# Token-tile gate loads, the first spectrum's row fix and Fourier's negated rows behind the filters' squares, in a one-layer Fourier and Hyena block

## The chip, the cores and the metric

The kernel runs on one core of one Trainium2 chip. The metric is the device time of one execution in microseconds (us). All arithmetic is in 32-bit floats; products that need full precision are made of three matmuls on a high and a low part of each operand.

TensorE (PE in the profile; PEld is its weight load), VectorE (DVE), ScalarE (ACT) and GpSimd (POOL) each work through a queue of their own, in order. Nearly all transfers are issued from the queue of SyncE (SP).

## The reference

One layer on x of 2048 tokens by 1024 channels, cut to what matters here:

```python
p = rmsnorm(x, g_mix) @ w_in                     # 512 Fourier channels, 3 x 512 Hyena channels
y_f = rmsnorm(fourier_mix(p[..., :512]), g_fourier)   # real part of a 2-D FFT, 8 groups of 64
u = short_conv(p[..., 512:])                     # 3 taps along the tokens
x1, x2, v = split(u, 3)
k = implicit_filters(...)                        # 2 orders x 512 channels, length 4096:
                                                 #   k * rsqrt(sum(k * k) + EPS)
k_freq = rfft(k)
z = v
for n, gate in enumerate((x1, x2)):
    z = gate * fft_long_conv(z, k_freq[:, n], long_d[n])
y_h = rmsnorm(z, g_hyena)
x = x + concat(y_f, y_h) @ w_out
x = x + square(relu(rmsnorm(x) @ w_fc1)) @ w_fc2
out = rmsnorm(x)
```

The change concerns the stretch in which the filters k are generated, squared, summed and Fourier transformed, with the Fourier group's FFT beside them, and the first load of v.

## The kernel before

The stages in order of time: projections with w_in and the short convolution (to about 408 us of the profiled execution), the filters' spectra with the Fourier group beside them (408 to 597 us), the long convolutions (597 to about 800 us), the output projection, and the two large products with w_fc1 and w_fc2.

**Filters.** There are 8 units, one for each pair of channel tile `ct` (4 of 128 channels) and order `n` (2). `filters` runs 44 steps; unit u is generated in steps 4u to 4u+3, one quarter k in each. `raw` makes the quarter on PE (L584, tile `pk`), `multiply` multiplies it by the decay on DVE (L589), and then two squares are made on ACT (L603, into `acc` for the very first and into `sqr` otherwise) and added on POOL (L605). After quarter 0 a row has to be moved first: ACT copies it to `lag0` (L598), DVE adds it and clears the place it came from (L599, L600). After quarter 3 POOL folds the sum (L607, L608). One step later `normalise` sums over partitions on PE (L613, `psum_k`), ACT takes the root (L617), DVE works out the reciprocal and a factor `dk` (L221 to L625), and `skip` uses that on PE (L636, L637, `pdk`). `stage1` transforms on PE (L654) with transposes on DVE (L658, `Gk`); `stage2` transforms on PE (L664), ACT copies the result out of PSUM (L667, tile `ks` of the filters, 3 buffers), and SP stores it to DRAM (L672, `spec`).

**Fourier.** In steps 0 to 10 the generator `fourier` is advanced between the units' work. From step 4 on, `rows(i)` transforms one or two rows: ACT first makes negated sines `neg` (L503) from the table `ff`, PE multiplies (L510 to L516; L511 and L515 read `neg`), ACT and DVE put the row together (L520 to L531), and SP stores it (L532, `yfd`). The first table, `ff0`, is loaded by SP when this stage begins.

**The gates and the first spectrum.** The short convolution left v, x1 and x2 in DRAM as `gd[0]` to `gd[2]`, each of 128 partitions x 16 token tiles x 512 channels. In steps 24 to 27 four loads (L722) bring `gd[0]` into the tile `zz`. In steps 30 to 37 DVE multiplies `zz` by the filters' norms (L725), channel tile after channel tile, two pieces of four token tiles in each instruction pair. The long convolutions then begin on PE with L774 (`pz`). Their first block needs the first spectrum: `spectrum(q)` loads it from DRAM (L760, tile `ks_6229` in the listings), and for q = 0 one row is fixed: ACT copies it (L763), POOL clears it in two places (L765). In the kernel before, the four calls for block 0 stand in a region of high priority as a whole.

**What sets the order.** Tile's scheduler orders each engine's queue by the program's order, by dependencies and by priority: inside `tc.high_priority(offset=n)` instructions are placed as if they stood n earlier. `behind(later, first)` adds an order without a semaphore: on one queue, `later` stands after `first`. PE's order is written out with `ordered`. The lists `acts`, `fetched` and `stored` hold instructions for later calls of `behind`; in the kernel before, `acts[0]` is the first copy to `lag0`, and `behind(fetched, stored[0])` puts the first spectrum's loads after the store of unit 3's spectrum.

Of the kernel before, what the change touches and what calls it, by code (L numbers as in the profile page):

```python
# [134 lines left out]
def hybrid_block(ctx: ExitStack, tc: tile.TileContext, A, out):  # L135
    nc = tc.nc
# [199 lines left out]
                w[h, k] = hi, lo  # L336
        return w

    line, acts, fetched, stored = [], [], [], []
    SINGLE = (5, 7)  # L340

    def doubled(i, q):
# [147 lines left out]
    def fourier(fp, uf, e1f, ffs):  # L490
        groups = [(0,)] + [(f, f + 1) for f in range(1, 17, 2)]
        G = fp.tile([P, 128, 32, 2], F32, tag="Gf", name="Gf")
        ufv = uf.rearrange("p t (b j) -> p t b j", b=2)
        for c in range(16):
            p = pa("pf1")
            ordered(nc.tensor.matmul(p, lhsT=e1f, rhs=ufv[:, :, :, 16 * c : 16 * c + 16], start=True, stop=True))
            yield turned(G, c, p.rearrange("p (x c e) -> p c e x", c=8, e=2))

        def rows(i):

            n, p = len(groups[i]), pa("pf2")
            neg = fp.tile([P, 2, P], F32, tag="neg", name="neg", bufs=2)[:, 0:n]
            behind([nc.scalar.mul(neg, ffs[i][:, :, 1], -1.0)], acts[0])  # L503
            for s, f in enumerate(groups[i]):
                co, si, ns = ffs[i][:, s, 0], ffs[i][:, s, 1], neg[:, s]
                a, b = p[:, 256 * s : 256 * s + 132], p[:, 256 * s + 132 : 256 * s + 256]
                gr, gi = (G[:, :, j].rearrange("p (c j) e -> p c j e", c=2) for j in (f, (16 + f) % 32))
                cos, sin = slice(0, 33), slice(33, 64)
                if f % 16 == 0:
                    ordered(nc.tensor.matmul(a, lhsT=co, rhs=gr[:, :, cos], start=True, stop=True))  # L510
                    ordered(nc.tensor.matmul(b, lhsT=ns, rhs=gr[:, :, sin], start=True, stop=True))  # L511
                else:
                    ordered(nc.tensor.matmul(a, lhsT=co, rhs=gr[:, :, cos], start=True, stop=False))
                    ordered(nc.tensor.matmul(a, lhsT=si, rhs=gi[:, :, cos], start=False, stop=True))
                    ordered(nc.tensor.matmul(b, lhsT=ns, rhs=gr[:, :, sin], start=True, stop=False))  # L515
                    ordered(nc.tensor.matmul(b, lhsT=co, rhs=gi[:, :, sin], start=False, stop=True))  # L516
            v = p.rearrange("p (s j) -> p s j", s=2)[:, 0:n]
            va = v[:, :, 0:132].rearrange("p s (c j) -> p s c j", c=2)
            sb = fp.tile([P, 2, 2, 62], F32, tag="sb", name="sb", bufs=2)[:, 0:n]
            nc.scalar.copy(sb, v[:, :, 132:256].rearrange("p s (c j) -> p s c j", c=2))  # L520

            row = fp.tile([P, 2, 388], F32, tag="row", name="row", bufs=2)[:, 0:n]

            def part(c, w):
                return row[:, :, c : c + 2 * w].rearrange("p s (c j) -> p s c j", c=2)

            nc.vector.tensor_add(part(0, 62), va[:, :, :, 0:62], sb)
            nc.vector.tensor_sub(part(132, 62), va[:, :, :, 0:62], sb)
            for c in (124, 256):
                nc.scalar.copy(part(c, 4), va[:, :, :, 62:66])  # L530
            nc.scalar.copy(row[:, :, 264:388], row[:, :, 0:124])  # L531
            nc.sync.dma_start(yfd[:, groups[i][0] : groups[i][0] + n, :], row)  # L532

        for i in range(len(groups)):
            rows(i)
            yield


    def filters(ctx, tp, fp, gp, zp, zzs, norms, emb, wo, e1k, f2, dk8, tabs, fourier_steps):
# [3 lines left out]
        p = pa("plongd")  # L543
# [3 lines left out]
        class Unit:  # L547
# [39 lines left out]
            def multiply(self, k, p, first=None):  # L587
# [7 lines left out]
                if k == 0:  # L595
                    zero, end = self.k[0:1, :, 0, :], self.k[32:33, :, 0, :]
                    lag0 = fp.tile([1, 128], F32, tag="lag0", name="lag0", bufs=2).rearrange("p (c j) -> p c j", c=8)
                    acts.append(nc.scalar.copy(lag0, end))  # L598
                    nc.vector.tensor_add(zero, zero, lag0)  # L599
                    nc.vector.memset(end, 0.0)  # L600
                for q in range(2):
                    sq = self.acc if k == 0 and q == 0 else fp.tile([P, 4, 128], F32, tag="sqr", name="sqr", bufs=2)
                    nc.scalar.square(sq.rearrange("p l (c j) -> p l c j", c=8), new[:, 4 * q : 4 * q + 4])  # L603
                    if sq is not self.acc:
                        nc.gpsimd.tensor_add(self.acc, self.acc, sq)  # L605
                if k == 3:
                    nc.gpsimd.tensor_add(self.acc[:, 0:2, :], self.acc[:, 0:2, :], self.acc[:, 2:4, :])  # L607
                    self.summed = nc.gpsimd.tensor_add(self.acc[:, 0, :], self.acc[:, 0, :], self.acc[:, 1, :])  # L608

            def normalise(self):  # L610

# [49 lines left out]
            def stage2(self, q):  # L661
                p = pa("pk2")
                for j in range(4):
                    ordered(nc.tensor.matmul(p[:, 128 * j : 128 * j + 128], lhsT=f2[:, 4 * q + j, :], rhs=self.G[:, :, 4 * q + j], start=True, stop=True))  # L664
                if q % 2 == 0:
                    self.ks = sp[0].tile([P, 8, 128], F32, tag="ks", name="ks", bufs=3)
                nc.scalar.copy(self.ks[:, 4 * (q % 2) : 4 * (q % 2) + 4, :], p.rearrange("p (f c) -> p f c", f=4))  # L667
                if q % 2:

                    n = 1 if self.i in SINGLE else 2  # L670
                    dst = kd[self.ct][self.n][0:n].rearrange("h p s x -> (p s) h x")[:, :, 512 * q - 512 : 512 * q + 512]
                    d = nc.sync.dma_start(dst, self.ks.rearrange("p (h f) c -> p h (f c)", h=1).broadcast_to([P, n, 1024]))  # L672
                    if self.i == 3:
                        stored[:] = [d]

        units = [Unit(i) for i in range(8)]
        decs, both, sp = {}, [], []
# [8 lines left out]
        for step in range(44):  # L686
# [29 lines left out]
                    for f in range(0, 16, 8):  # L716
                        nc.sync.dma_start(tabs[j][:, f : f + 8], A["f2"][:, 16 * j + f : 16 * j + f + 8])
            if step in LOAD:
                cs = slice(128 * LOAD[step], 128 * LOAD[step] + 128)
                if not zzs:  # L720
                    zzs.append(zp.tile([P, NT, 512], F32, tag="zz", name="zz"))
                nc.sync.dma_start(zzs[0][:, :, cs], gd[0][:, :, cs])  # L722
            for j, q in SCALE.get(step, ()):
                z = zzs[0][:, 4 * q : 4 * q + 4, 128 * j : 128 * j + 128]
                behind([nc.vector.tensor_mul(z, z, norms[:, j : j + 1, :].broadcast_to([P, 4, 128]))], flipped)  # L725
# [3 lines left out]
    def hyena(hp, wp, rp, zz, e1, b1, f2, a2, work):  # L729
# [6 lines left out]
        class Block:  # L736
# [9 lines left out]
            def spectrum(self, q):  # L746
# [10 lines left out]
                else:  # L757
                    ks = hp.tile([P, 2, 4, 128], F32, tag="ks", name="ks", bufs=4)
                src = kd[self.ct][self.n].rearrange("h p s x -> (h p) s x")[:, :, 512 * q : 512 * q + 512]
                fetched[:] = [nc.sync.dma_start(ks.rearrange("p s f c -> p s (f c)"), src)]  # L760
                if q == 0:

                    nc.scalar.copy(ks[64:65, 0, 0, :], ks[64:65, 1, 0, :])  # L763
                    for h in (0, 64):
                        nc.gpsimd.memset(ks[h : h + 1, 1, 0, :], 0.0)  # L765
                return ks

            def first(self, c):
# [48 lines left out]
        LAST = ((0,), (1, 2), (3, 4), (5, 6), (7,))  # L817
        FIRSTS = ((0, 1), (2, 3), (4,), (5,), (6,), (7,), (), ())
        blocks = [Block(n, ct) for n in range(2) for ct in range(4)]
        with tc.high_priority(offset=4000):  # L820
            for k in range(4):
                blocks[0].ahead[k] = blocks[0].spectrum(k)
                behind(fetched, stored[0])
        for k in range(4):
            nc.sync.dma_start(a2[:, 8 * k : 8 * k + 8], A["a2"][:, 8 * k : 8 * k + 8])
        for c in range(8):
# [743 lines left out]
```

## Time and profile before

| | |
|---|---|
| median of 3 runs | 2268.5 us (2267.15 to 2270.2) |
| profiled execution | 2269.76 us, span of its instructions 2268.0 us |
| PE busy | 2200.2 us, 97% |
| DVE busy | 1474.9 us, 65% |
| ACT busy | 1075.2 us, 47% |
| POOL busy | 767.3 us, 34% |
| mean granted clock of PE | 0.991 |

In the views, a row of the timeline holds start, duration, engine, line, operation, output and input, and in brackets how long the engine stood idle ahead of it and what released it. "issue" there is time in which the engine waited for nothing that the profile shows. In the views by windows, PEclk is the granted clock (1.00 is full speed) and the DMA share is the mean busy share of 16 DMA engines; it can pass 1 where their packets overlap. Matmuls are pipelined, so a start is firmer than an end.

### The profile page before, as it was taken

What the parts mean: (1) busy time and instruction counts of PE and PEld (TensorE: products, weight loads), DVE (VectorE), ACT (ScalarE), POOL (GpSimd) and SP (SyncE); (2) the same over time, 40 slices, a digit from 0 to 9 for tenths busy, and PEclk for the clock granted to TensorE, in tenths of its full rate; (3) what the DMA queues carried; (4) which work ended last, traced back from release to release, by engine and by line L of the source; (5) the groups of instructions that cost most, each with busy time, mean ns of one, the idle gap of its engine ahead of it and who ended that gap; (6) DMA issues with size and microseconds to landing.
All of it is one profiled execution on the core that took longest, in us unless ns stands there. A gap on an engine that the chain in (4) does not pass through costs nothing.

```text
span 2268.0 us, 34541 instructions
## 1 busy us (share of the span) xinstructions
PE 2200.2 (97%) x12881; PEld 1799.0 (79%) x12881; DVE 1474.9 (65%) x2196; ACT 1075.2 (47%) x1788; POOL 767.3 (34%) x583
## 2 busy tenths in 40 slices
PE   8999899998999989998999989999999999999998
PEld 6888788675788868887888878888888888888886
DVE  6999766775688764466444475444466666966667
ACT  6545211354455645446555565555533333533333
POOL 3434322454266602236555556555300000000000
PEclk9999999999999999999999999999999999999999
DMA  8535987579887756567444464444498766866631
GB/s 273 179 133 175 336 286 248 190 264 332 299 287 215 242 149 181 177 209 241 153 154 153 152 243 163 154 153 154 144 350 324 241 190 201 299 195 195 189 117 75
DMA packets 296633, 477.00 MB, mean 210 GB/s; under 512 B 17477, under 2 KB 141583, under 8 KB 292241
## 3 DMA queue, kind: packets, MB, share of 16 engines
q1 hardware_dynamic: 290513, 459.34, 61.2%
q10 hardware_dynamic: 5952, 15.46, 2.0%
q8 instruction: 101, 1.65, 0.3%
q14 instruction: 67, 0.55, 0.1%
HBM read 309.36 MB, written 168.00 MB: 210 GB/s over the span
## 4 chain that ended last, share of the span: by engine, by line
PE 86%; DVE 5%; ACT 2%; DMA 2%; POOL 2%; issue 2%; SPq 0%; ACTq 0%; DVEq 0%; POOLq 0%
PE p2u L210 5%; PE p2u L211 5%; PE p2u L212 5%; PE p1u L210 5%; PE p1u L212 5%; PE p1u L211 5%; PE pu L212 4%; PE pu L211 4%; PE pu L210 4%; PE p2v L210 3%; PE p2v L211 3%; PE p2v L212 3%; PE pz L781 2%; PE pz L774 2%; PE pv L797 2%; PE p1v L210 2%
## 5 line engine op out<-in xcount | busy, mean ns | idle before, releaser
L196 ACT CAST qahm<-ra 128x1024 fp32r<-128x1024 f32 x110 | 115.9, 1053 | 345.6 <-PE p2u L211 172.0
L197 DVE TENSOR_TENSOR qalm<-ra,qahm 128x1024 fp32r<-128x1024 f32 x110 | 134.6, 1224 | 154.2 <-ACT qahm L196 152.4
L1342 POOL TENSOR_TENSOR acc<-acc,gfin 128x512 f32<-128x512 f32 x4 | 5.1, 1279 | 631.6 <-DMA out<-acc 624.4
L211 PE MATMUL pu<-wl,xh 128*128 128x512 f32 x512 | 201.5, 394 | 6.9 <-DVE wl L197 6.5
L210 PE MATMUL pu<-wh,xh 128*128 128x512 f32 x512 | 204.0, 399 | 1.8 <-ACT wh L199 1.8
L212 PE MATMUL pu<-wh,xl 128*128 128x512 f32 x512 | 201.1, 393 | 0.9 <-DVE xl L197 0.9
L211 PE MATMUL p2u<-qblm,qahm 128*128 128x512 f32 x504 | 196.1, 389 | 0.0
L210 PE MATMUL p2u<-qbhm,qahm 128*128 128x512 f32 x504 | 195.8, 389 | 0.0
L212 PE MATMUL p2u<-qbhm,qalm 128*128 128x512 f32 x504 | 195.8, 389 | 0.0
L197 DVE TENSOR_TENSOR qblm<-rb,qbhm 128x1024 fp32r<-128x1024 f32 x110 | 134.0, 1218 | 2.2 <-ACT qbhm L196 1.8
L411 POOL TENSOR_TENSOR acc<-acc,cw 128x512 f32<-128x512 f32 x45 | 59.9, 1332 | 204.7 <-DVE acc L388 201.4
L196 ACT CAST ahm<-s 128x512 fp32r<-128x512 f32 x124 | 76.7, 621 | 98.3 <-PE p1v L211 53.3
L197 POOL TENSOR_TENSOR alm<-W,ahm 128x512 fp32r<-128x512 f32 x63 | 87.9, 1396 | 96.8 <-ACT ahm L196 90.4
L211 PEld LDWEIGHTS pu<-wl,xh 128*128 128x128 f32 x512 | 97.2, 190 | 28.4 <-DVE wl L197 6.9
L196 ACT CAST qbhm<-rb 128x1024 fp32r<-128x1024 f32 x110 | 115.3, 1048 | 4.2 <-DMA rb<-in_w_fc 2.7
L210 PEld LDWEIGHTS pu<-wh,xh 128*128 128x128 f32 x512 | 97.0, 189 | 22.7 <-ACT wh L199 2.2
L212 PEld LDWEIGHTS pu<-wh,xl 128*128 128x128 f32 x512 | 97.1, 190 | 22.4 <-DVE xl L197 2.3
L788 POOL TENSOR_TENSOR zs<-zs,ks 128x512 f32<-128x512 f32 x64 | 83.3, 1302 | 82.2 <-ACT zs L785 75.7
L210 PEld LDWEIGHTS p2u<-qbhm,qahm 128*128 128x128 f32 x504 | 94.6, 188 | 20.1 <-issue 0.3
L212 PEld LDWEIGHTS p2u<-qbhm,qalm 128*128 128x128 f32 x504 | 94.6, 188 | 19.7
L211 PEld LDWEIGHTS p2u<-qblm,qahm 128*128 128x128 f32 x504 | 94.6, 188 | 19.4
L210 PE MATMUL p1u<-bm,ahm 128*128 128x512 f32 x252 | 100.7, 400 | 9.3 <-ACT ku L1204 9.3
(376 smaller groups left out, 6124.1 us busy)
## 6 DMA issues: line engine op xcount, KB each, us to landing
W<-in_w_fc SPq DMA_DIRECT2D x66, 512.0 KB, 4.6
ks<-spec SPq DMA_DIRECT2D x64, 512.0 KB, 4.2
rb<-td SPq DMA_DIRECT2D x64, 512.0 KB, 4.1
ra<-a1m SPq DMA_DIRECT2D x56, 512.0 KB, 3.5
ra<-a0m SPq DMA_DIRECT2D x54, 512.0 KB, 4.2
spec<-ks SPq DMA_DIRECT2D x24, 1024.0 KB, 5.3
rb<-in_w_fc SPq DMA_DIRECT2D x46, 512.0 KB, 4.9
f<-in_w_fc SPq DMA_DIRECT2D x16, 1024.0 KB, 6.6
```

What stands on the lines that cost most here:

```text
L196: nc.scalar.copy(hi, src)
L197: (eng or nc.vector).tensor_sub(lo, src, hi)
L210: a = nc.tensor.matmul(o, lhsT=lh, rhs=rh, start=start, stop=False, skip_group_check=more)
L211: nc.tensor.matmul(o, lhsT=lh, rhs=rl, start=False, stop=False, skip_group_check=more)
L212: return a, nc.tensor.matmul(o, lhsT=ll, rhs=rh, start=False, stop=stop, skip_group_check=more)
L411: nc.gpsimd.tensor_add(m1, m1, cw[:, 3, :])
L774: nc.tensor.matmul(p[:, 256 * sp : 256 * sp + 256], lhsT=e1[:, sp, :], rhs=zz[:, :, lo : lo + 16], start=True, stop=True)
L781: nc.tensor.matmul(p[:, 128 * j : 128 * j + 128], lhsT=f2[q // 4][:, 4 * (q % 4) + j, :], rhs=self.G[:, :, 4 * q + j], start=True, stop=True)
L788: nc.gpsimd.tensor_mul(zs, zs, ks[:, 1])
L797: nc.tensor.matmul(p[:, 128 * j : 128 * j + 128], lhsT=a2[:, 4 * q + j, :], rhs=self.y[q][:, j, :], start=True, stop=True)
L1342: nc.gpsimd.tensor_mul(acc[i][:, c], acc[i][:, c], gfin[:, c])
```

## The change

Three things are changed.

1. The four loads of `gd[0]` take four token tiles with all channels each, instead of all token tiles with 128 channels each. A partition's part was 16 runs of 128 floats (512 bytes); it is now 4 token tiles of 512 floats (2 KB each) that lie one after another. Bytes, number of loads and places in SP's queue are the same.
2. The first spectrum's fix (ACT's L763, POOL's two L765) is placed behind the last copy out of PSUM on ACT and the last sum on POOL. Only the loads of the spectrum keep the high priority.
3. Fourier's `neg` is placed behind the last square of unit 0 instead of behind the first copy to `lag0`.

```diff
-    line, acts, fetched, stored = [], [], [], []
+    line, acts, fetched, stored, summed = [], [], [], [], []
...
-            behind([nc.scalar.mul(neg, ffs[i][:, :, 1], -1.0)], acts[0])
+            behind([nc.scalar.mul(neg, ffs[i][:, :, 1], -1.0)], acts[-1])
...
-                    acts.append(nc.scalar.copy(lag0, end))
+                    nc.scalar.copy(lag0, end)
...
-                    nc.scalar.square(sq.rearrange("p l (c j) -> p l c j", c=8), new[:, 4 * q : 4 * q + 4])
+                    a = nc.scalar.square(sq.rearrange("p l (c j) -> p l c j", c=8), new[:, 4 * q : 4 * q + 4])
+                    if step < 4:
+                        acts.append(a)
...
-                    self.summed = nc.gpsimd.tensor_add(self.acc[:, 0, :], self.acc[:, 0, :], self.acc[:, 1, :])
+                    summed[:] = [nc.gpsimd.tensor_add(self.acc[:, 0, :], self.acc[:, 0, :], self.acc[:, 1, :])]
...
-                nc.scalar.copy(self.ks[:, 4 * (q % 2) : 4 * (q % 2) + 4, :], p.rearrange("p (f c) -> p f c", f=4))
+                last = nc.scalar.copy(self.ks[:, 4 * (q % 2) : 4 * (q % 2) + 4, :], p.rearrange("p (f c) -> p f c", f=4))
...
+                    acts.append(last)
...
-                cs = slice(128 * LOAD[step], 128 * LOAD[step] + 128)
+                ts = slice(4 * LOAD[step], 4 * LOAD[step] + 4)
...
-                nc.sync.dma_start(zzs[0][:, :, cs], gd[0][:, :, cs])
+                nc.sync.dma_start(zzs[0][:, ts], gd[0][:, ts])
...
-                fetched[:] = [nc.sync.dma_start(ks.rearrange("p s f c -> p s (f c)"), src)]
+                with tc.high_priority(offset=4000) if self is blocks[0] and q < 4 else ExitStack():
+                    fetched[:] = [nc.sync.dma_start(ks.rearrange("p s f c -> p s (f c)"), src)]
...
-                    nc.scalar.copy(ks[64:65, 0, 0, :], ks[64:65, 1, 0, :])
+                    behind([nc.scalar.copy(ks[64:65, 0, 0, :], ks[64:65, 1, 0, :])], acts[-1])
...
-                        nc.gpsimd.memset(ks[h : h + 1, 1, 0, :], 0.0)
+                        behind([nc.gpsimd.memset(ks[h : h + 1, 1, 0, :], 0.0)], summed[0])
...
-        with tc.high_priority(offset=4000):
-            for k in range(4):
-                blocks[0].ahead[k] = blocks[0].spectrum(k)
-                behind(fetched, stored[0])
+        for k in range(4):
+            blocks[0].ahead[k] = blocks[0].spectrum(k)
+            behind(fetched, stored[0])
```

The orders of PE and DVE are the same in both kernels, instruction for instruction. ACT, POOL and SP differ at the places that follow.

ACT where the filters' generation begins (unit 0, then the first Fourier rows), before:

```order
L598 COPY lag_3674<-k 1x128
L603 ACTIVATE sqr<-k 128x512
L503 ACTIVATE neg<-ff_3612 128x128
L503 ACTIVATE neg<-ff 128x256
L603 ACTIVATE acc<-k 128x512
L603 ACTIVATE sqr<-k 128x512 x4
L520 COPY sb<-pf_3840 128x124
L503 ACTIVATE neg<-ff 128x256
L603 ACTIVATE sqr<-k 128x512 x2
```

And there in the changed kernel:

```order
L598 COPY lag_3674<-k 1x128
L603 ACTIVATE sqr<-k 128x512
L603 ACTIVATE acc<-k 128x512
L603 ACTIVATE sqr<-k 128x512 x6
L503 ACTIVATE neg<-ff_3612 128x128
L503 ACTIVATE neg<-ff 128x256
L520 COPY sb<-pf_3840 128x124
L503 ACTIVATE neg<-ff 128x256
```

All eight squares of unit 0 now stand ahead of the first negated sines; the two `neg` of the first rows stood ahead of seven of them.

ACT where unit 7 begins (step 28; `ks_6229` is the first spectrum, `lag_5677` belongs to unit 7), before:

```order
L667 COPY ks<-pk_5627 128x512
L667 COPY ks<-pk_5634 128x512
L763 COPY ks_6229<-ks_6229 1x128
L598 COPY lag_5677<-k 1x128
L603 ACTIVATE sqr<-k 128x512
```

The same place in the changed kernel:

```order
L669 COPY ks<-pk_5627 128x512
L669 COPY ks<-pk_5634 128x512
L598 COPY lag_5677<-k 1x128
L603 ACTIVATE sqr<-k 128x512
```

The fix has left this place; it now stands after the last of the copies from PSUM (L669 in the changed kernel's numbering), ahead of the first instruction of the long convolutions on ACT. On POOL the two clearings stood between the sums of unit 6 and unit 7, and now stand after unit 7's. In SP's queue only the form of the four gate loads differs (128x16x128 before, 128x2048 now).

## The prediction

> **What bounds the kernel now.** I read the page's chain of work first, then the waits, then the timeline of the two stretches where the chain leaves PE.
>
> ```profile
> PE 2200.2 (97%) x12881; PEld 1799.0 (79%) x12881; DVE 1474.9 (65%) x2196; ACT 1075.2 (47%) x1788; POOL 767.3 (34%) x583
> PE 86%; DVE 5%; ACT 2%; DMA 2%; POOL 2%; issue 2%; SPq 0%; ACTq 0%; DVEq 0%; POOLq 0%
> ```
>
> PE is busy 97% of the span and carries 86% of the chain, so a microsecond counts only where PE stands idle or runs slowly. The change touches two such places. The waits of the stretch from 500 to 612 us (engine, waiting tile and line, releaser: total, times, longest) show the larger one:
>
> ```profile
> DVE k L599 <- ACT lag L598: 8.6, 3, 7.9
> PE pk L654 <- DVE vk L615: 5.4, 1, 5.4
> ```
>
> and the timelines of ACT, DVE and PE there show how it arises:
>
> ```profile
> 548.35 0.29 ACT L763 COPY ks<-ks 1x128 f32<-1x128 f32 x1 [10.68 <-DMA ks<-spec]
> 548.66 0.30 ACT L598 COPY lag<-k 1x128 f32<-1x128 f32 x1
> ```
>
> ```profile
> 539.90 1.22 DVE L589 TENSOR_TENSOR k<-pk,dec 128x1024 f32<-128x1024 f32 x1 [3.21 <-PE pk L584]
> 549.53 1.32 DVE L658 STREAM_TRANSPOSE Gk<-pk 128x512 f32<-128x512 f32 x2
> ```
>
> ```profile
> 542.75 1.09 PE L584 MATMUL pk<-wo,emb 64*32 64x128 f32 x57
> 545.19 0.42 PE L584 MATMUL pk<-wo,emb 64*32 64x128 f32 x7 [1.35 <-issue]
> 550.99 1.96 PE L654 MATMUL pk<-k,e1k 64*32 64x512 f32 x16 [5.38 <-DVE vk L615]
> 552.89 2.94 PE L664 MATMUL pk<-Gk,f 128*128 128x128 f32 x16
> 556.38 1.16 PE L584 MATMUL pk<-wo,emb 64*32 64x128 f32 x64
> 564.39 1.09 PE L654 MATMUL pk<-k,e1k 64*32 64x512 f32 x16
> 565.42 2.05 PE L664 MATMUL pk<-Gk,f 128*128 128x128 f32 x16
> ```
>
> The row fix L763 waits on ACT 10.68 us for the first spectrum's load. Behind it stands unit 7's copy L598, whose input was ready at 541.1 (539.90 + 1.22). DVE's transposes L658 stand behind that copy's successor, and PE's next L654 needs their PSUM buffer. PE idles 5.38 us and then does the same 16 + 16 matmuls in 4.9 us (1.96 + 2.94) that take 3.1 us at 564.39 (1.09 + 2.05): its clock has fallen.
>
> The smaller place is where the filters begin:
>
> ```profile
> 424.03 0.62 ACT L503 ACTIVATE neg<-ff 128x128 f32<-128x128 f32 x2 [6.34 <-issue]
> 424.56 0.61 ACT L603 ACTIVATE acc<-k 128x512 f32<-128x512 f32 x1
> 436.90 1.28 ACT L617 ACT_TABLE_LOAD   x1
> ```
>
> ```profile
> 425.25 9.43 POOL L605 TENSOR_TENSOR acc<-acc,sqr 128x512 f32<-128x512 f32 x7 [16.93 <-ACT acc L603]
> ```
>
> ```profile
> 427.39 1.22 DVE L589 TENSOR_TENSOR k<-pk,dec 128x1024 f32<-128x1024 f32 x1 [0.36 <-PE pk L584]
> 440.79 0.27 DVE L625 TENSOR_SCALAR dk<-vk,nw_k,longd 128x1 f32<-128x1 f32 x1
> ```
>
> ```profile
> 427.27 0.49 PE L510 MATMUL pf<-Gf,ff 128*128 128x132 f32 x2
> 427.60 0.38 PE L511 MATMUL pf<-Gf,neg 128*128 128x124 f32 x2
> 436.13 0.58 PE L613 MATMUL psum_k<-ones,acc 128*128 128x1 f32 x2 [3.27 <-POOL acc L608]
> 442.86 1.16 PE L584 MATMUL pk<-wo,emb 64*32 64x128 f32 x64
> ```
>
> The two `neg` hold ACT for 6.34 us (their table's load is the only input that is new there), POOL's seven adds start only at 425.25, and PE waits 3.27 us for the folded sum.
>
> What an idle PE costs beside the idle time is read by windows (length, busy time of each engine, granted clock, DMA share, GB/s):
>
> ```profile
> 435.50:442.30 6.80, 6.17 (x83) 5.59 (x84) 3.45 (x11) 4.77 (x11) 3.21 (x4) 0.51 0.70 211
> 548.10:555.00 6.90, 4.01 (x26) 2.37 (x27) 5.23 (x13) 3.84 (x9) 1.89 (x4) 0.52 1.04 406
> 568.60:572.00 3.40, 2.10 (x24) 1.25 (x25) 3.06 (x9) 0.20 (x1) 1.16 (x2) 1.00 0.95 293
> 828.00:831.40 3.40, 0.79 (x6) 0.76 (x7) 2.42 (x11) 2.02 (x7) 0.00 (x0) 0.98 0.40 86
> 831.40:834.80 3.40, 3.40 (x12) 2.86 (x11) 1.44 (x3) 3.08 (x9) 0.00 (x0) 0.52 0.98 298
> ```
>
> After each of the two stalls PE runs at half clock for 6.8 us. The starts 435.5, 548.1 and 831.4 lie a whole number of 3.41 us steps apart (33, then 83), so I take the clock as decided on a fixed raster: a step with PE busy 0.79 of 3.40 us is followed by half clock, a step with 2.10 is not.
>
> **The change, part by part.**
>
> *Row fix behind the last copy.* L763 leaves the queue ahead of L598. Then L598 runs at 541.15, L599 and L600 end near 542.0, the two transposes near 543.4, and L654 can start when PE has finished its L584, at 545.6 (545.19 + 0.42). Gain: the idle 5.38 us, and the clock loss, 4.9 - 3.1 = 1.8 us. Together 7.2 us; PE's L584 at 556.38 should come 7.2 us earlier against its own step's start. In its new place, behind the last L667, it takes the same 0.29 us, and the load has landed by 548.35, long before; POOL's clearings waited for the same load, and no row of the chain waits for them. Late next at this spot is PE itself. Bounds: 5.4 (if the clock fell all the same) and 8.6 (if the 1.35 us of issue goes too); I take 7.2.
>
> *`neg` behind unit 0's squares.* The squares are ready when DVE's products are; the last product ends at 428.6 (427.39 + 1.22), the last two squares near 429.8, POOL's last two adds near 432.0 (1.35 each, from 9.43 / 7), and with 1.45 us for folding (436.13 less 425.25 + 9.43) `psum_k` could start at 433.45. But now the first `neg` comes at 429.75 and is done at about 430.1, and PE's L511, which ran at 427.60, must wait for it: a new stall of about 2.45 us, with all of PE's queue behind it. Removed: 3.27 us idle and half of PE's 6.17 busy us at half clock, 3.0, together 6.3. Added: 2.5 for the new stall and, since ACT's table load at 436.90 hardly moves (it stands behind a square of unit 1) and DVE's `dk` (now ready at 441.06) comes at about 439.3, some 0.85 us of PE waiting for `dk`. Left: 2.95 us, if the new stall does not drop the clock. A stall of 2.45 us inside one raster step leaves 0.95 of 3.4 us busy, near the 0.79 that was followed by half clock; split in halves it leaves 2.2, like the 2.10 that was not. The nearer row by length is 828.00 (2.6 us idle), so I take a drop, one step of half clock, 1.7 us of work lost, of which the wait for `dk` takes up a little: 1.5 us gained. Bounds: 0 (half clock for 6.8 us) and 2.95.
>
> The rule on this in the Trainium skill (TensorE: Matmul & The Clock Gate, Part 1: The HAM clock gate) is that the clock halves after at least one idle window of about 3.4 us. By that rule a stall of 2.45 us would leave it whole, and the sum would be that of the first rival. The trace disagrees at 828.00, where a step that was not idle throughout was followed by half clock.
>
> *Gate loads in longer runs.* Bytes and places are unchanged. What they cost now:
>
> ```profile
> 496.00:511.00 15.00, 15.00 (x383) 11.15 (x381) 9.90 (x20) 8.49 (x19) 9.48 (x9) 1.00 0.83 305
> 511.00:545.00 34.00, 29.62 (x667) 21.59 (x660) 17.32 (x28) 14.23 (x29) 17.23 (x16) 1.00 1.06 339
> 548.00:559.00 11.00, 8.01 (x122) 4.97 (x123) 6.65 (x15) 5.39 (x13) 4.21 (x5) 0.69 0.91 357
> ```
>
> ```profile
> 525.08 1.08 PE L654 MATMUL pk<-k,e1k 64*32 64x512 f32 x12 [1.82 <-issue]
> 539.02 0.74 PE L584 MATMUL pk<-wo,emb 64*32 64x128 f32 x34 [1.41 <-issue]
> ```
>
> While the four loads run (511 to 545) a full DMA share moves 320 GB/s (339 / 1.06); without them 367 (305 / 0.83) and 392 (357 / 0.91). At 367 the 11.5 MB of that stretch need a share of 0.92 instead of 1.06. Nothing waits for these loads: DVE's scaling begins 25 us after the last one is issued. But all three of PE's idle times with no releaser, 1.82, 1.41 and the 1.35 above, 4.6 us in all, fall into this stretch, and none into 496 to 511. I infer that PE then waits for instructions that come by the same DMA engines. A share of 0.92 lies at two fifths between 0.83 and 1.06, and with 2 us less time for the same bytes at about half; so half of the 4.6 goes: 2.3 us. Bounds: -1.8 (one more stall as long as the longest, since the new runs' effect on them is not in this trace) and 4.6.
>
> *Sum.* 7.2 + 1.5 + 2.3 = 11.0 us. The profiled execution took 2269.76 us (span 2268.0, 1.8 around it), 1.3 above the median of 2268.5. From the profiled execution the sum gives 2258.8, from the median 2257.5. The runs shown lie 3 us apart, so I forecast from the median: 2257.5.
>
> After 600 us the order of all engines is as before and every wait is relative to PE, so I expect what is gained by 597 us to be kept to the end.
>
> **Rivals.**
>
> *The clock stays whole at the new stall.* The stall may fall across two raster steps. Then Fourier's part gives 2.95: 2268.5 - 7.2 - 2.95 - 2.3 = 2256.0. For it: the 568.60 row; against it: the 828.00 row.
>
> *The longer runs change nothing on PE.* Stalls without a releaser stay as they are: 2268.5 - 7.2 - 1.5 = 2259.8. For it: the share stays above 0.9. The Trainium skill (DMA: Bandwidth & Descriptors, Specifications) puts the least transfer for line rate at 512 B, by which 512-byte runs would lose nothing. The 320 against 367 GB/s of the rows disagree with it.
>
> *All of the issue time goes.* 2268.5 - 7.2 - 1.5 - 4.6 = 2255.2. For it: none of it lies outside the loads' stretch; against it: the share stays above that of 496 to 511.
>
> *The pause is paid back.* PE's stall at 545 lets the DMA queues drain (share 0.91 from 548). Without it, stores of the spectra could fall behind, ACT's copies L667 (3 buffers) would wait for them, and PE would idle 5.4 us later instead of here. Then 2268.5 - 1.5 - 1.8 = 2265.2, within 0.2%. The transfers (KB each, median us to landing, whole run):
>
> ```profile
> ks<-spec SPq DMA_DIRECT2D x64, 512.0 KB, 4.2
> spec<-ks SPq DMA_DIRECT2D x24, 1024.0 KB, 5.3
> ```
>
> Against it: from 541 on, four loads of the first spectrum and four stores, 6.3 MB, need 17 us at 367 GB/s; the PE steps that make these stores end at 564.4 now and would at 557, 16 us after 541, and three buffers stand between.
>
> *A token-tile load comes too late (slower).* The first channel tile's scaling needed the first load alone, and now needs all four:
>
> ```profile
> 535.03 0.52 SPq L722 DMA_DIRECT2D zz<-gates  x1
> 565.51 3.20 DVE L725 TENSOR_TENSOR zz<-zz,norms 128x512 f32<-128x512 f32 x2
> ```
>
> The second pair of scalings would run about 554.5, the last load is issued about 531: 23 us. Beyond that each microsecond of delay holds DVE, and PE behind its transposes; the kernel gets slower when the load takes over 34 us, and by over 0.2% (4.5 us, about what a measurement of this kernel can tell from no change) from 39 us, 2273.0. No load in this stretch shows anything like it.
>
> **How the numbers follow.** Chances: forecast (2257.5) 0.40, clock whole (2256.0) 0.17, runs change nothing (2259.8) 0.20, all issue time goes (2255.2) 0.10, pause paid back (2265.2) 0.10, late load (2273) 0.03. The range: the bounds together give 2268.5 - 7.2 - 2.95 - 4.6 = 2253.75 at the best and 2268.5 - 7.2 - 0 + 1.8 = 2263.1 at the worst; with the runs' own scatter 2253.5 to 2263.5, which leaves out the last two cases, 0.13. Faster by over 0.2% (below 2264.0): 0.87; within 0.2%: 0.10; slower: 0.03.
>
> **What would show it.** Right: ACT has no wait for `ks<-spec` ahead of `lag`, PE's L654 of that step follows its L584 without idle time and takes 1.1 us; `psum_k` follows PE's rows without a wait, PE waits about 2.5 us at the first L511 for `neg`; half clock once instead of twice there; idle times without a releaser in the loads' stretch about halved. Wrong: a wait of ACT's L667 for a store of `spec`, or of DVE's L725 for `zz<-gates`, or PE waiting longer than 3.3 us at L511, for then the table's load and not the squares sets `neg`.

## The result, and the profile after

The changed kernel takes 2264.04 us (median of 20 runs, 2260.66 to 2269.15), beside 2268.95 us for the kernel before on the same chip (median of 20 runs, 2264.23 to 2272.93). The ratio is 0.9977, with a 95% interval from 0.9969 to 0.9984: 4.9 us faster, where 11.0 were forecast. The time lies 0.5 us above the top of the range. The profiled execution took 2262.79 us, 1.8 of it around its span, at a mean granted clock of 0.993.

The page of the changed kernel (busy time by engine, chain by engine):

```profile
span 2261.0 us, 34543 instructions
PE 2199.3 (97%) x12881; PEld 1798.0 (80%) x12881; DVE 1475.1 (65%) x2196; ACT 1074.8 (48%) x1788; POOL 767.8 (34%) x583
PE 87%; DVE 4%; DMA 3%; ACT 2%; issue 2%; POOL 1%; SPq 0%; ACTq 0%; DVEq 0%; POOLq 0%
```

The work is the same; what moved is idle time of PE and its clock. In the listings of the changed kernel the lines behind the sums stand two to four higher: the squares' adds are L607, `psum_k` L615, `pdk` L638, stage 1 L656, stage 2 L666, the copies out of PSUM L669, the stores L674, the gate loads L725, the first spectrum's loads L764 and its fix L767.

**The larger place.** Timeline of PE where unit 7 begins, changed kernel:

```profile
542.01 1.09 PE L584 MATMUL pk<-wo,emb 64*32 64x128 f32 x57
544.73 0.31 PE L584 MATMUL pk<-wo,emb 64*32 64x128 f32 x4 [1.62 <-issue]
...
544.88 1.12 PE L656 MATMUL pk<-k,e1k 64*32 64x512 f32 x14
545.93 2.05 PE L666 MATMUL pk<-Gk,f 128*128 128x128 f32 x16
...
548.53 1.16 PE L584 MATMUL pk<-wo,emb 64*32 64x128 f32 x64
```

and of ACT, at unit 7's copy and where the fix now stands:

```profile
540.42 0.30 ACT L598 COPY lag<-k 1x128 f32<-1x128 f32 x1 [2.94 <-DVE k L589]
...
591.06 0.29 ACT L767 COPY ks<-ks 1x128 f32<-1x128 f32 x1
```

The copy L598 waits for its own input and not for a load; stage 1 follows L584 at once, at full clock (1.12 us for the last 14 of its 16 matmuls and 2.05 for the 16 of stage 2; before, each 16 took 1.96 and 2.94). From the L584 x57 to the next whole L584 x64 PE needs 6.52 us (542.01 to 548.53) where it needed 13.63 (542.75 to 556.38). Without the idle time put down to issue in it (1.62 and 1.35) that is 4.90 beside 12.28.

**The smaller place.** PE, and ACT's last squares of unit 0 with the first `neg` behind them, changed kernel:

```profile
430.13 0.48 PE L511 MATMUL pf<-Gf,neg 128*128 128x124 f32 x2 [2.35 <-ACT neg L503]
...
435.34 0.28 PE L615 MATMUL psum_k<-ones,acc 128*128 128x1 f32 x2
...
439.55 0.38 PE L638 MATMUL pdk<-ident,dk 128*1 128x128 f32 x2 [0.85 <-ACT sqr L603]
```

```profile
428.73 1.15 ACT L603 ACTIVATE sqr<-k 128x512 f32<-128x512 f32 x2 [3.57 <-DVE k L589]
429.79 0.60 ACT L503 ACTIVATE neg<-ff 128x128 f32<-128x128 f32 x2
```

The new stall at L511, the disappearance of the wait at `psum_k` and the new wait at `pdk` came at the places and in the sizes foretold (2.45, 0 and 0.85). No half clock follows. (The releaser at `pdk` is named as ACT's square; its input `dk` ends on DVE at 439.40.)

**The loads' stretch.** Idle times of PE without a releaser (beside the one of 1.62 us above; the first lies ahead of the loads), and the window that answers to the one of 339 GB/s:

```profile
445.11 0.52 PE L584 MATMUL pk<-wo,emb 64*32 64x128 f32 x18 [0.96 <-issue]
517.23 0.54 PE L584 MATMUL pk<-wo,emb 64*32 64x128 f32 x21 [0.51 <-issue]
524.88 1.08 PE L656 MATMUL pk<-k,e1k 64*32 64x512 f32 x12 [2.17 <-issue]
538.28 0.74 PE L584 MATMUL pk<-wo,emb 64*32 64x128 f32 x34 [0.86 <-issue]
```

```profile
511.00:545.00 34.00, 28.85 (x668) 20.93 (x674) 18.82 (x37) 16.31 (x35) 17.72 (x16) 1.00 1.02 392
```

They did not halve: 6.12 us in all between 440 and 560 us, 4.58 before. The transfers did get quicker, 384 GB/s at a full share (392 / 1.02) instead of 320, and PE had nothing of it.

### The profile page after: what moved, and what is told of

It is laid out like the page before. It is cut to its first block, busy times and chain, and to the rows that moved or that the text cites. A ratio compares the mean times of both kernels' runs of the same rounds, so it can differ in the third digit from the quotient of the medians.

```text
span 2261.0 us, 34543 instructions
## 1 busy us (share of the span) xinstructions
PE 2199.3 (97%) x12881; PEld 1798.0 (80%) x12881; DVE 1475.1 (65%) x2196; ACT 1074.8 (48%) x1788; POOL 767.8 (34%) x583
## 3 DMA queue, kind: packets, MB, share of 16 engines
q8 instruction: 101, 1.65, 0.3%
## 4 chain that ended last, share of the span: by engine, by line
PE 87%; DVE 4%; DMA 3%; ACT 2%; issue 2%; POOL 1%; SPq 0%; ACTq 0%; DVEq 0%; POOLq 0%
PE p2u L212 5%; PE p2u L210 5%; PE p2u L211 5%; PE p1u L210 5%; PE p1u L212 5%; PE p1u L211 5%; PE pu L212 4%; PE pu L211 4%; PE pu L210 4%; PE p2v L212 3%; PE p2v L210 3%; PE p2v L211 3%; PE pz L778 2%; PE pk L666 2%; PE p1v L210 2%; PE p1v L212 2%
## 5 line engine op out<-in xcount | busy, mean ns | idle before, releaser
L196 ACT CAST ahm<-W 128x512 fp32r<-128x512 f32 x94 | 57.8, 617 | 101.7 <-PE p1u L211 99.5
```

Source lines behind the costliest of these rows:

```text
L196: nc.scalar.copy(hi, src)
```

## Experiments

The theory that the traces suggested: the row fix carries the whole gain; `neg` and the loads carry none, `neg` because it trades a wait for another, the loads because PE's idle times of this stretch do not hang on the DMA engines. The rivals: each of the three edits gives its share of the gain, or one of them costs what another brings. Ratios are to the kernel before on the same chip, with 95% intervals; a ratio is estimated from the single executions and is not the quotient of the two medians beside it.

**Each edit alone.** Gate loads alone:

```diff
-                cs = slice(128 * LOAD[step], 128 * LOAD[step] + 128)
+                ts = slice(4 * LOAD[step], 4 * LOAD[step] + 4)
...
-                nc.sync.dma_start(zzs[0][:, :, cs], gd[0][:, :, cs])
+                nc.sync.dma_start(zzs[0][:, ts], gd[0][:, ts])
```

> Only the gate loads' form is changed; the fix and neg stay as before. Theory A (the forecast): the idle times of PE without a releaser between 511 and 545 us fall from 4.6 to about 2.3 us, and the kernel is 2.3 us faster (ratio 0.999). Theory B (from the profile of the changed kernel, where these idle times came to 6.1 us): they do not hang on the length of the runs; they stay at 4 to 6 us and the time is the same within 1.5 us (ratio 1.000). Both: PE's wait of about 5.4 us for the row fix and of 3.3 us for psum_k stay.

Measured: 2264.05 us (12 runs) against 2270.06, ratio 0.9978 (0.9967 to 0.9989). So the loads alone do gain some 5 us. The trace shows by what. PE of this kernel (numbered as the kernel before) at unit 7, and ACT's row fix:

```profile
544.10 0.42 PE L584 MATMUL pk<-wo,emb 64*32 64x128 f32 x7 [1.62 <-issue]
546.79 1.96 PE L654 MATMUL pk<-k,e1k 64*32 64x512 f32 x16 [2.27 <-DVE vk L615]
```

```profile
544.15 0.29 ACT L763 COPY ks<-ks 1x128 f32<-1x128 f32 x1 [7.62 <-DMA ks<-spec]
```

The fix still stands ahead of the copy L598, but the spectrum that it waits for lands at 544.15 instead of 548.35, and PE's stall falls from 5.38 to 2.27 us. Why the load is earlier shows in SP's queue. Before (start, then how long the queue was held at the issue):

```profile
522.23 7.06 SPq L672 DMA_DIRECT2D spec<-ks  x1
...
529.95 5.02 SPq L672 DMA_DIRECT2D spec<-ks  x1
...
535.64 5.34 SPq L672 DMA_DIRECT2D spec<-ks  x1
541.03 3.77 SPq L760 DMA_DIRECT2D ks<-spec  x4
```

Gate loads alone:

```profile
521.35 0.37 SPq L672 DMA_DIRECT2D spec<-ks  x1
...
532.61 0.37 SPq L672 DMA_DIRECT2D spec<-ks  x1
533.03 3.27 SPq L760 DMA_DIRECT2D ks<-spec  x4
```

Behind each of the last three gate loads of 512-byte runs SP is held 5.0 to 7.1 us at the next store (2.6 us behind the first); behind one of long runs 0.36 or 0.37 us. So the first spectrum's loads are issued 8 us earlier (533.03 for 541.03).

Row fix alone (with the clearings; `neg` behind the first `lag0` copy, loads in 512-byte runs):

```diff
-    line, acts, fetched, stored, summed = [], [], [], [], []
+    line, acts, fetched, stored, summed, lags = [], [], [], [], [], []
...
-            behind([nc.scalar.mul(neg, ffs[i][:, :, 1], -1.0)], acts[-1])
+            behind([nc.scalar.mul(neg, ffs[i][:, :, 1], -1.0)], lags[0])
...
-                    nc.scalar.copy(lag0, end)
+                    lags.append(nc.scalar.copy(lag0, end))
...
-                ts = slice(4 * LOAD[step], 4 * LOAD[step] + 4)
+                cs = slice(128 * LOAD[step], 128 * LOAD[step] + 128)
...
-                nc.sync.dma_start(zzs[0][:, ts], gd[0][:, ts])
+                nc.sync.dma_start(zzs[0][:, :, cs], gd[0][:, :, cs])
```

(This diff and the later ones are against the changed kernel.)

> Only the row fix and POOL's clearings are moved. Theory A: PE's idle 5.4 us before L654 and the half clock after it go, 7.2 us (ratio 0.9968); psum_k still waits 3.3 us and its half clock stays. Theory B: the same at that place, but idle times without a releaser grow by 1 to 2 us since the pause no longer gives them time: 5 to 6 us in all (ratio 0.9975).

Measured: 2260.96 us (6 runs) against 2270.06, ratio 0.9963 (0.9949 to 0.9977). One edit gives all of the gain. PE of this kernel:

```profile
433.96 0.38 PE L615 MATMUL psum_k<-ones,acc 128*128 128x1 f32 x2 [0.66 <-POOL acc L610]
```

```profile
538.89 1.09 PE L584 MATMUL pk<-wo,emb 64*32 64x128 f32 x57
542.15 0.31 PE L584 MATMUL pk<-wo,emb 64*32 64x128 f32 x4 [2.17 <-issue]
...
545.96 1.16 PE L584 MATMUL pk<-wo,emb 64*32 64x128 f32 x64
```

The step is 7.07 us, 4.90 without its issue time: the same 4.90 as in the changed kernel. The first row is the surprise. `neg` stands here where it stood before, but `psum_k` waits 0.66 us and not 3.27. ACT of this kernel shows the cause:

```profile
421.79 0.62 ACT L503 ACTIVATE neg<-ff 128x128 f32<-128x128 f32 x2 [5.11 <-issue]
```

The first `neg` runs 2.2 us earlier than in the profile of before (424.03), and ACT went on to the squares that much earlier. SP issued the load of its table as much earlier. Before, then here:

```profile
417.42 0.33 SPq L185 DMA_DIRECT2D ff<-in_ff  x1
```

```profile
415.19 0.33 SPq L185 DMA_DIRECT2D ff<-in_ff  x1
```

In both, `neg` starts 6.6 us behind that issue. What moves the issue from one execution to the next stays open.

`neg` alone (the changed kernel with the gate loads and the fix as before: the four calls of `spectrum` under high priority, the fix without `behind`):

> Only neg is placed behind unit 0's squares. Theory A: 1.5 us faster if the clock falls at the new stall of 2.4 us at L511, 2.95 us if not (ratio 0.9993 to 0.9987), all kept to the end. Theory B: the lead of 2.7 us at pdk is used up by 541 us, since the row fix there ends with a load whose landing the DMA queues set and not PE: under 1 us faster (ratio 0.9996 to 1.000).

Measured: 2268.35 us (12 runs) against 2270.06, ratio 0.9998 (0.9986 to 1.001): no difference shown. PE of this kernel:

```profile
429.82 0.49 PE L511 MATMUL pf<-Gf,neg 128*128 128x124 f32 x2 [2.35 <-ACT neg L503]
...
550.43 1.96 PE L656 MATMUL pk<-k,e1k 64*32 64x512 f32 x16 [7.97 <-DVE vk L617]
```

The same stall of 2.35 us, here followed by half clock from 430.9. And the stall of unit 7 is 2.6 us longer than before (7.97 for 5.38): PE reached it earlier and the load did not.

**Fix and `neg` together, 512-byte runs.**

> The changed kernel with the gate loads' form of before (512-byte runs). Theory A: slower than the changed kernel by 2.3 us, so 8.7 to 10.2 us faster than before (ratio 0.996). Theory B: the same as the changed kernel within 1.5 us, 4 to 7 us faster than before (ratio 0.997 to 0.998), with 4 to 6 us of idle times without a releaser.

Measured: 2261.72 us (6 runs) against 2270.06, ratio 0.9966 (0.9953 to 0.9979). Leaving the long runs away costs nothing that shows, though alone they gained 5 us: the fix no longer stands on ACT ahead of anything that waits for the load. The stall at L511 is 2.35 us again, with half clock behind it. In windows on the clock's raster, the step ahead of that fall here and the step after it:

```profile
428.10:431.51 3.41, 1.47 (x13) 1.47 (x14) 0.93 (x3) 2.56 (x9) 2.02 (x2) 1.00 0.00 0
431.51:434.92 3.41, 3.41 (x73) 2.81 (x71) 0.74 (x2) 1.40 (x7) 1.72 (x3) 0.50 0.18 63
```

and the step of the changed kernel that holds most of the same stall, with the step after it:

```profile
428.39:431.80 3.41, 1.67 (x14) 1.67 (x15) 0.73 (x3) 2.66 (x9) 2.22 (x2) 1.00 0.00 0
431.80:435.21 3.41, 3.41 (x85) 3.09 (x84) 1.87 (x3) 1.54 (x6) 1.51 (x3) 1.00 0.29 101
```

The changed kernel's step is placed by its fall at 786.79 us, 105 steps of 3.413 us after 428.39. PE busy 1.47 of 3.41 us was followed by half clock, 1.67 was not; in the kernel with `neg` alone it is 1.11, with half clock behind it. By the rule of the Trainium skill (TensorE: Matmul & The Clock Gate, Part 1: The HAM clock gate) no stall of 2.35 us should have halved the clock, since that takes a wholly idle window; here and in the kernel with `neg` alone it did.

**The changed kernel again.**

> The changed kernel once more, on one chip with the next ones. Theory C (from the first four experiments): the fix gives its 7 us, neg about nothing, since the wait that it removes was 0.7 to 3.3 us and the one it adds 2.35 us with a fall of the clock in most executions; the longer runs about nothing beside the fix. So 5 to 7 us faster than before (ratio 0.997 to 0.998). In its profile L511 waits 2.35 us again. Theory A (the forecast): 11 us (ratio 0.995).

Measured: 2262.8 us (11 runs) against 2269.64, ratio 0.9974 (0.9963 to 0.9984); its trace repeats the first one: 2.35 us at L511, 0.85 at `pdk`, no half clock there, and 4.66 us of issue time between 440 and 560 us.

**`neg` behind the third quarter's squares**, so that two squares are left behind it:

```diff
-            behind([nc.scalar.mul(neg, ffs[i][:, :, 1], -1.0)], acts[-1])
+            behind([nc.scalar.mul(neg, ffs[i][:, :, 1], -1.0)], acts[5])
```

> The changed kernel, but neg stands behind the squares of unit 0's third quarter instead of its last. Theory C: L511 no longer waits, psum_k waits 0.7 us as where the table landed early, dk is ready at 437.2, so pdk comes 2.3 us earlier than in the changed kernel and the clock does not fall there; 2.3 to 3.3 us faster than the changed kernel (ratio to before 0.996 to 0.9965). Rival D: what is gained at 440 is lost again by 545 in idle times without a releaser, and the time is that of the changed kernel.

Measured: 2262.19 us (12 runs) against 2269.64, ratio 0.9969 (0.9958 to 0.9981). PE of this kernel:

```profile
433.43 0.38 PE L615 MATMUL psum_k<-ones,acc 128*128 128x1 f32 x2 [0.65 <-POOL acc L610]
437.45 0.38 PE L638 MATMUL pdk<-ident,dk 128*1 128x128 f32 x2 [0.55 <-ACT sqr L603]
```

No stall at L511, and from PE's first L584 of this stage (408.51) to `pdk` 28.94 us instead of the changed kernel's 30.94. The 2.0 us are plain in the trace; the whole run does not show them beyond its scatter.

**Less traffic: unit 3's spectrum stored once** (2 MB less stored in the loads' stretch; its second copy is made in the long convolutions, as for units 5 and 7):

```diff
-    SINGLE = (5, 7)
+    SINGLE = (3, 5, 7)
...
-                if i in (1, 2) and q % 2:
+                if i in (1, 2, 3) and q % 2:
```

> The changed kernel, but unit 3's spectrum is stored once (0.5 MB a step instead of 1 MB, in steps 24 to 27, beside the gate loads) and doubled later from DRAM, beside the long convolutions. Theory E: PE's idle times without a releaser grow with what the DMA engines have in flight; with 2 MB less of some 13 they fall from 6.1 to 3 us or less, and the kernel is 2 to 4 us faster than the changed one, if the later copies cost nothing. Rival F: they come with PE's own stream of instructions and stay at 4 to 6 us; same time as the changed kernel.

Measured: 2264.96 us (12 runs) against 2269.64, ratio 0.9972 (0.9959 to 0.9985). The issue time came to 6.34 us, with the longest single one of all executions, and half clock after it:

```profile
545.52 0.31 PE L584 MATMUL pk<-wo,emb 64*32 64x128 f32 x4 [2.99 <-issue]
```

**More traffic: each gate load followed by a copy of the same 1 MB from DRAM to DRAM** (4 MB in all; the copies are read by nobody):

```diff
+    spare = scratch("spare", [P, NT, 512])
...
-                nc.sync.dma_start(zzs[0][:, ts], gd[0][:, ts])
+                a = nc.sync.dma_start(zzs[0][:, ts], gd[0][:, ts])
+                behind([nc.sync.dma_start(spare[:, ts], gd[0][:, ts])], a)
```

> The changed kernel with 4 MB more of transfers: behind each gate load the same token tiles are copied once more, from DRAM to an unused place in DRAM. The order of some copies on ACT moves with it, so only the idle times are read. Theory E: idle times without a releaser between 505 and 555 us come to 9 us or more (5 us in the changed kernel). Rival F: 4 to 6 us.

Measured: 2266.53 us (one run) against 2269.64. Issue time 6.26 us, 5.6 of it between 505 and 555 us. What the traffic does cost stands elsewhere, at a copy out of PSUM (lines one higher here):

```profile
518.56 0.87 PE L585 MATMUL pk<-wo,emb 64*32 64x128 f32 x21 [2.60 <-issue]
...
561.54 3.19 PE L667 MATMUL pk<-Gk,f 128*128 128x128 f32 x16 [2.96 <-ACT ks L670]
```

With 2 MB less and with 4 MB more the issue time is nearly the same. But the mean DMA share between 511 and 545 us is 0.99 and 1.01 in these two kernels, and 1.02 in the changed one: the engines were as busy in all three, so these runs cannot tell what less busy ones would give. The wait at 561.54 is the "pause paid back" of the prediction.

**Fix, `neg` behind the third quarter, 512-byte runs** (the edit of `neg` above, and the loads as before):

> The row fix moved, neg behind the third quarter's squares, gate loads in 512-byte runs as before. Theory C: beside the fix the form of the loads is worth nothing, and neg at this place takes 2 us from the path from the first pk to pdk (28.9 us, against 30.9 with neg behind all squares and 28.9 to 33.7 with neg as before): 7 to 9 us faster than before (ratio 0.996 to 0.997). Theory A, by which the longer runs give 2.3 us: 2 us slower than the same kernel with long runs.

Measured: 2261.28 us (6 runs) against 2268.87, ratio 0.9966 (0.9954 to 0.9978); `psum_k` waits 0.66 us, `pdk` comes 28.95 us after the first L584.

**Three repeats for the scatter of the smaller place**: the row fix alone, the kernel before, and the gate loads alone.

> The row fix alone once more, on one chip with the kernel above. Theory C: 6 to 8 us faster than before (ratio 0.9965 to 0.9973); the wait for psum_k lies somewhere between 0.7 and 3.3 us, by the landing of the first table, and with 3.3 us the clock falls for two steps. Theory A: 7.2 us, with a wait of 3.3 us each time.

> The kernel before, one more profile. Theory C: the first neg starts anywhere between 421.8 and 424.1 us and the wait for psum_k follows it, between 0.7 and 3.3 us; SP is held 3 us or more at stores of spec between 525 and 541 us and issues the first spectrum's loads after 540. Theory A: 3.3 us and 5.4 us of waiting as in the first profile.

> The longer runs alone, one more profile. Theory C: SP issues each store of spec between 525 and 541 us in under 0.5 us, the first spectrum's loads at 533 to 535, their landing at 544 to 545 and PE's wait behind the row fix 2 to 3 us instead of 5.4 to 8. Rival: that was chance, and the wait is 5 us or more.

Measured: the fix alone 2261.9 us (7 runs) against 2268.87, ratio 0.9968 (0.9958 to 0.9979); the kernel before, one run, 2270.73; the loads alone, one run, 2267.45. The `psum_k` rows of the fix alone, of the kernel before and of the loads alone, in this order, and behind each the row of stage 1 at unit 7 where it waits:

```profile
437.20 0.38 PE L615 MATMUL psum_k<-ones,acc 128*128 128x1 f32 x2 [2.21 <-POOL acc L610]
```

```profile
436.52 0.59 PE L613 MATMUL psum_k<-ones,acc 128*128 128x1 f32 x2 [2.70 <-POOL acc L608]
...
552.46 1.96 PE L654 MATMUL pk<-k,e1k 64*32 64x512 f32 x16 [5.59 <-DVE vk L615]
```

```profile
435.56 0.38 PE L613 MATMUL psum_k<-ones,acc 128*128 128x1 f32 x2 [1.65 <-POOL acc L608]
...
546.26 1.96 PE L654 MATMUL pk<-k,e1k 64*32 64x512 f32 x16 [2.29 <-DVE vk L615]
```

The fix alone waits 2.21 us at `psum_k` in this execution and 0.66 in the other: same program, but SP issued the table's load 9.2 us after the stage's first L584 here and 6.2 in the other. The wait of the row fix, in contrast, repeats within about 0.2 us (5.38 and 5.59; 2.27 and 2.29).

In this execution of the fix alone, ACT then waits for a store, unit 7's last squares come late, and PE waits for their sum:

```profile
556.74 1.07 ACT L669 COPY ks<-pk 128x512 f32<-128x512 f32 x2 [4.55 <-DMA spec<-ks]
```

```profile
563.49 0.38 PE L615 MATMUL psum_k<-ones,acc 128*128 128x1 f32 x2 [3.90 <-POOL acc L610]
```

The kernel with fix and `neg` and 512-byte runs does the same (4.35 and 3.92 us). In the other two executions with the fix and 512-byte runs PE waits 2.52 and 2.62 us there, in the kernel before and the changed one 2.4. So in two of four the pause is paid back in part, by some 1.4 us.

## Why the prediction was right and wrong

**The row fix: right.** Foretold 7.2 us, bounds 5.4 to 8.6. The step of unit 7 without its issue time takes 12.28 and 12.26 us in the two executions of the kernel before; with the fix moved it takes 4.89 or 4.90 in seven executions of five programs, and in that with the extra copies; only the one with the spectrum stored once differs (6.52, half clock). That is 7.4 us. Both parts, the idle 5.4 and the clock loss behind it, went. In the changed kernel nothing was paid back at the stores: unit 7's `psum_k` waits 2.41 and 2.42 us in its two executions, for 2.43 before. With 512-byte loads some 1.4 us were, in two executions of four, as the last rows above show.

**`neg`: the mechanism right, the term mis-sized.** What was added came as worked out (2.35 us, and 0.77 to 0.85), in every profile that has it there. What failed is the 6.3 us removed: a wait of 3.27 us, and a half clock of 6.8 us, were read from one execution and taken for the kernel's. They hang on when one table is there. With `neg` as before the first `neg` starts 12.75 to 15.43 us after the stage's first L584, the `psum_k` wait is 3.27, 2.70, 2.21, 1.69, 1.65 and 0.66 us in six executions, and the half clock behind it lasts 6.8, 6.8, 3.4, 3.4, 3.4 and 0 us. From the first L584 to `pdk` that makes 33.65, 33.1, 31.7, 31.0, 30.9 and 28.9 us, 31.5 in the mean. With `neg` moved it is 30.9 in four executions and 32.4 in the two where the clock halved, 31.4 in the mean. So the term is 0.1 us by these means, of executions that scatter by 4.7 us. The ratio 0.9998 for `neg` alone can't tell it from 1.5 us, and there unit 7's longer wait takes up what is gained; but the fix with `neg` (0.9966) is no faster than the fix without it (0.9963 and 0.9968), all with 512-byte runs. The profile of before showed the longest of the six; its 2.7 us against the changed kernel's 30.94 are the luck of that pair. The lower bound, 0, was right about the mean and too high for a single pair: against the best landing the edit loses 2 us.

**The clock at the new stall: the argument right, the choice between its two cases not.** The clock stayed whole in four of six executions and halved in two, and what decides is how the stall is split over the raster's steps, as the windows above show: the emptiest step holds 1.11 and 1.47 us of PE where the clock halved, 1.67 to 2.18 where it did not. The forecast had taken the halving for the likelier; the profile of the changed kernel is the first rival's case. It moves the sum by 1.5 us and did not decide the result.

**The gate loads: wrong.** The step that failed is "At 367 the 11.5 MB of that stretch need a share of 0.92 instead of 1.06", and with it the half of the idle time that was to go, 2.3 us. The share stayed at 1.02: SP, held less, issued the next transfers earlier, and 13.3 MB (392 GB/s for 34 us) passed in the stretch instead of 11.5. Between 440 and 560 us the idle time without a releaser sums to 4.58, 4.65, 2.99, 5.37, 5.33, 5.11 and 3.54 us in seven executions with 512-byte runs (mean 4.5) and 6.12, 4.66, 4.88, 2.97, 5.51, 6.34 and 6.26 in seven with long ones (mean 5.2, and 4.8 without the last two, whose traffic differs). This is the rival "the longer runs change nothing on PE" (2259.8), which was given 0.20.

The inference beside that step, that PE waits for instructions, holds. The idle time falls at the same matmuls in nearly every program (L584 with 18, 21, 34 and 4 or 7 instructions of its group left, stage 1 with 12). Counted over the trace's records of matmuls, weight loads and PE's semaphore instructions, all 56 of these idle times, in 14 executions, lie whole multiples of 256 instructions apart. And each time a packet of 16 KB, in the DMA queue that the trace calls `instruction`, ends 1.1 to 1.6 us before PE goes on. For the 2.17 us that end at 524.88 in the changed kernel it runs from 522.49 to 523.39 us; the DMA view from 522.4 to 523.5 (packets, MB, share) has it:

```profile
q8 instruction: 1, 0.02, 5.1%
```

For the five blocks of 256 that PE enters between about 515 and 547 us, this packet begins 4.0 us (median) after PE entered the block before, with runs of either length; between 455 and 485 us, where the DMA share is 0.62 to 0.66, it begins 0.8 to 1.0 us after. That fits packets held up by busy DMA engines, but no run brought the share of the loads' stretch below 0.99, so it is not shown by a change. Two places do answer to the edits, while the sum does not: L584 with 21 left waits in all seven executions with long runs, longest with the extra copies, and in none with 512-byte runs; and L584 with 18 left waits (0.5 to 1.0 us) in the nine executions where PE waited under 1 us for unit 0's `psum_k` and in none of the other five, so that a part of what is gained there is lost again at the next block.

What the longer runs really do, the prediction did not have: they free SP's queue by 8 us, and so bring the first spectrum earlier. Alone this takes 3.1 us off the stall that the row fix makes: unit 7's step without issue time is 9.85 and 8.82 us with the loads alone, for 12.28. That is 2.4 to 3.5 of the 5.0 us measured (2.5 to 7.5 by the interval); the rest of the traces' difference lies in the path to the first `pdk` (30.96 and 30.9 us, for 33.65 and 33.1), which the table's load sets, so for the rest of the medians' gain I have no row. But the row fix, moved, removes the same stall from the other end. The gains of the two edits do not add: 0.9978 and 0.9963 alone, 0.9977 together (with `neg`).

**The sum.** In the pair of profiles: fix 7.4, `neg` 2.7, more issue time -1.5; 0.7 us are lost in rows between the two places that I did not follow further, and 0.9 behind 600 us, where half clock falls at other places from one execution to the next; together the 7.0 us by which the spans differ. In the medians, where the luck of a pair averages out, it is the fix alone: 7.4 by the traces; by the differences of the medians 4.9 and 6.8 for the changed kernel, 7.0 and 9.1 for the fix alone. Whether the difference between these is real stays open: the four ratios with the fix and 512-byte runs are 0.9963, 0.9966, 0.9966 and 0.9968, the three with the fix, long runs and no other traffic than before 0.9977, 0.9974 and 0.9969. All of the first lie below all of the second, by 0.1 to 1.4 per mille, but every interval overlaps every other, and no row shows a loss beyond 0.6 us of issue time (4.8 in the mean of the first four profiles, 5.4 in that of the other three).

The late token-tile load did not come; the stores that fall behind came in part, in two executions with 512-byte loads and with the extra copies. No version tried beats the fix alone: with `neg` behind the third quarter it is 0.9966.

## What to carry to other kernels

A short wait that ends with the landing of a load is a sample, not a property: before it is put into a sum, see it in a second execution, or put its whole spread into the bounds. Ask of each edit which wait it shortens, and if two edits shorten the same one, count it once. Idle time "without a releaser" can be a wait for instructions: count the engine's instructions between two such places, and look for a packet of the `instruction` queue ahead of them. And a quicker transfer leaves the DMA engines no less busy when more transfers stand behind it in the queue.

## What the runs showed of the hardware

- A load of 1 MB in 512-byte runs holds the queue that issued it: in the kernel before SP stood 2.6, 7.1, 5.0 and 5.3 us at the store behind each of the four, and 0.36 or 0.37 us when the same bytes came in 8 KB per partition. It is not the load's own row that shows it (0.5 to 1.0 us) but the one behind it.
- A full DMA share moved 320 GB/s with the 512-byte loads and 384 with the long ones in the same stretch, which holds not quite the same transfers. The packets of the two traces there say it directly: one of 512 bytes took 29.8 ns in the mean and one of 8 KB 324 ns, which is 275 and 404 GB/s for 16 engines. The Trainium skill (DMA: Bandwidth & Descriptors, Specifications) counts 512 bytes as enough for line rate; the rows here disagree.
- The clock's raster held across whole executions: in the changed kernel the half clock starts at 233.83, 786.79 and 824.33 us lie 162 and 11 steps of 3.413 us apart. On this raster, in all 14 executions (from 20 to 2240 us), each of the 81 steps at full clock with PE busy 1.47 us or less was followed by half clock, and none with 1.92 us or more was. Of the 51 between, 28 were: there the busy time alone does not decide (1.67 kept the clock in the changed kernel, 1.72 lost it with the gate loads alone).
- PE's instructions came in blocks of 256, one packet of 16 KB each. Where the packet ended late, PE stood idle until 1.1 to 1.6 us after it, 0.15 to 2.99 us at a time, and the profile names no releaser.
